# Retention with both heads' zero-padded queries in one full-array product

## The chip, the cores and the metric

The kernel runs on one core of a Trainium2 chip. Its engines are TensorE (PE; its weight loads are shown apart as PEld), VectorE (DVE), ScalarE (ACT), GpSimd (POOL) and SyncE (SP), which here issues nearly all DMA transfers. The metric is the device time of one execution in microseconds: before, the median of three runs is 3554.91 us (3552.26 to 3559.05).

## The reference

A decoder trunk of two layers on a stream of 16 + 512 = 528 positions with 1024 channels. Each layer normalises, projects once, runs four token mixers (RWKV-7, Mamba-2 SSD, retention, RG-LRU), merges them by gates, and ends with a SwiGLU network. Only retention is touched, so only it is shown: 8 heads, keys and queries of 64, values of 128, chunks of positions.

```python
q = rope(q.reshape(bsz, t_len, H, DK), pos)
k = rope(k.reshape(bsz, t_len, H, DK), pos) * (DK ** -0.5)
...
scores = jnp.einsum('bclhd,bcshd->bchls', qc, kc) * intra
y_in = jnp.einsum('bchls,bcshe->bclhe', scores, vc)
kv = jnp.einsum('bclhd,hl,bclhe->bchde', kc, k_dec, vc)

def step(r_state, kv_c):
    return chunk_dec * r_state + kv_c, r_state

_, r_prev = lax.scan(step, jnp.zeros(...), jnp.moveaxis(kv, 1, 0))
y_x = jnp.einsum('bclhd,hl,cbhde->bclhe', qc, q_dec, r_prev)
y = (y_in + y_x).reshape(bsz, nc * L, H, DV)[:, pad:]
y = y * lax.rsqrt(jnp.mean(y * y, axis=-1, keepdims=True) + NORM_EPS)
return jax.nn.silu(g) * y.reshape(bsz, t_len, RET_V_WIDTH)
```

`rope` rotates pairs of channels by the position, `intra` is a causal mask with a decay per head, and `r_prev` is the state of 64 x 128 that a head hands from chunk to chunk.

## The kernel before, in words

All activations are kept transposed: channels on partitions, the 528 positions along the free dimension. A projection (`dense`, line 240) multiplies a 1024 x 128 block of weights with the stream. Weights and activations are each split into a rounded part and a remainder (tiles `whi` and `wlo`, `hh` and `hl`), so that each of eight blocks takes three products, on two halves of 264 columns. These dense products make up most of TensorE's work. The small products of the mixers are plain float32; each of those is issued as two instructions, so one such product counts as 2 in the timeline and as 1 in the order.

The order of the work is set by `layer`. RWKV-7 is a serial loop over eight pairs of heads. Each step builds products (line 853), inverts small triangular matrices on VectorE (lines 903 and 905, 31 rounds), sends the result through DRAM (lines 906, 912, 913), brings it back to TensorE (line 936), and runs a chain over nine chunks (lines 955, 960, 971) to the outputs (lines 988, 990). Between the parts, `fill` pulls pieces from a generator `others`, which runs the other mixers and the gates. Each piece ends with a `yield` of its estimated microseconds, and `fill` pulls until its share is used up. A scheduler then orders the instructions by priority; reads of PSUM are marked `soon()` and go ahead. Each engine works through its own list in order.

Retention is the generator `ret`, one call for two heads (j = 0 to 3 in each of two layers, eight units in all). It uses six chunks of 88 positions.

- `rope` (lines 388 to 404) makes the rotated keys `kr` and queries `qr`, with the decay multiplied in (line 401). Two heads of 64 channels share the 128 partitions: head e has rows 64e to 64e + 63.
- `transposes` (line 414) makes `kT` and, per head, `vT`, positions on partitions.
- Scores, line 458: per head and chunk a product of 64 rows, 88 by 88. Line 461 applies the causal mask.
- States, line 471: per chunk and head a product into 64 of the 128 partitions; lines 476 to 479 form the running state `R` on VectorE.
- Outputs, lines 490 and 492: per head and chunk, values times scores (88 rows) plus state times query (64 rows), accumulated in one PSUM region. `group` holds the instructions of one bank in order.
- Line 496 squares the output, line 497 multiplies it by the gate, `sums` (lines 279 to 285) adds the squares over partitions with a rounded part and a remainder, lines 500 and 502 turn the sum into a reciprocal root, line 503 applies it, and `spill` writes the result to DRAM.

The second half runs for one head completely before the other. Its small products go through `psm`, a pool of two PSUM banks, which other parts use too.

Of the kernel before, what the change touches and what calls it, by code (L numbers as in the profile page):

```python
# [21 lines left out]
T = 528  # L22
H2 = 264
# [6 lines left out]
CL = 88  # L30
NC = 6

RWKV0, SSM0, RET0, LRU0, GATE0 = 0, 3328, 6416, 9488, 11536
# [56 lines left out]
class _Em:  # L90
# [294 lines left out]
        o, w = COFF[name] - NCST0, dict(CCOLS)[name]  # L385
        return self.rc[rows, o:o + w]

    def rope(self, ps, p, tag, dec, j):
        nc = self.nc
        x = self.t(p, T, "rx", bufs=1)  # L390
        xs = self.t(p, T, "rxs", bufs=1)
        with self.soon():
            nc.scalar.activation(v2(x), ps, AF.Copy)
        for b in range(4):
            o = (b ^ 1) * 32
            nc.sync.dma_start(out=xs[b * 32:b * 32 + 32], in_=x[o:o + 32])
        r = self.t(p, T, tag)
        nc.vector.tensor_tensor(out=x, in0=x, in1=self.rcc("cos"), op=MUL)
        nc.vector.tensor_tensor(out=xs, in0=xs, in1=self.rcc("sin"), op=MUL)
        nc.vector.tensor_tensor(out=x, in0=x, in1=xs, op=ADD)  # L400
        nc.vector.tensor_tensor(
            out=r.rearrange("p (c x) -> p c x", c=NC), in0=x.rearrange("p (c x) -> p c x", c=NC),
            in1=self.rcc(dec)[:, j * CL:(j + 1) * CL].unsqueeze(1).broadcast_to([128, NC, CL]), op=MUL)
        return r

    def transposes(self, src, use):

        nc = self.nc
        k = src.shape[0]
        for a in range(2):  # L410
            ps = self.bank(self.psm)[:CL, :3 * k]
            for c in range(3):
                o = (3 * a + c) * CL
                nc.tensor.transpose(ps[:, c * k:c * k + k], src[:, o:o + CL], self.c("ident")[:k, :k])  # L414
            with self.soon():
                use(ps, a)

    def ret(self, l, j, X, p, out):
        nc = self.nc
        src = ("w_in", l)  # L420
        kr = self.rope(self.dense(src, RET0 + 512 + j * 128, X), p, "kr", "kdec", j)
        yield DENSE
        qr = self.rope(self.dense(src, RET0 + j * 128, X), p, "qr", "qdec", j)
# [17 lines left out]
        kT = self.t(p, [NC, 128], "kT", parts=CL)  # L441

        def halfview(t, a):
            return t[:, 3 * a:3 * a + 3].rearrange("p c x -> p (c x)")

        self.transposes(kr, lambda ps, a: nc.scalar.activation(halfview(kT, a), ps, AF.Copy))
        vTs, scs = [], []
        for e in range(2):
            vT = self.t(p, [NC, 128], f"vT{e}", parts=CL)
            self.transposes(vs[e], lambda ps, a: nc.scalar.activation(halfview(vT, a), ps, AF.Copy))  # L450
            vTs.append(vT)
            sc = self.t(p, T, f"sc{e}", parts=CL)
            hr = slice(e * 64, e * 64 + 64)
            for a in range(2):
                ps = self.bank(self.psm)[:CL, :H2]
                for c in range(3):
                    o = a * H2 + c * CL
                    nc.tensor.matmul(ps[:, c * CL:(c + 1) * CL], kr[hr, o:o + CL], qr[hr, o:o + CL],
                                     start=True, stop=True)
                with self.soon():  # L460
                    nc.vector.tensor_tensor(
                        out=sc[:, a * H2:(a + 1) * H2].rearrange("p (c x) -> p c x", c=3),
                        in0=ps.rearrange("p (c x) -> p c x", c=3),
                        in1=self.c("cau", slice(0, CL)).unsqueeze(1).broadcast_to([CL, 3, CL]), op=MUL)
            scs.append(sc)
            yield 2.2
        R = self.t(p, [NC, 128], "R")
        for c in range(NC - 1):
            ps = self.bank(self.psm)[:, :128]
            for e in range(2):  # L470
                nc.tensor.matmul(ps[e * 64:e * 64 + 64], kT[:, c, e * 64:e * 64 + 64], vTs[e][:, c],
                                 start=True, stop=True)
            cd = self.rcc("cdec")[:, j:j + 1]
            with self.soon():
                if c == 0:
                    nc.vector.tensor_scalar(out=R[:, 1], in0=ps, scalar1=cd, scalar2=None, op0=MUL)
                else:
                    nc.vector.tensor_tensor(out=R[:, c + 1], in0=R[:, c], in1=ps, op=ADD)
                    nc.vector.tensor_scalar(out=R[:, c + 1], in0=R[:, c + 1], scalar1=cd, scalar2=None, op0=MUL)
        for e in range(2):  # L480
            hr = slice(e * 64, e * 64 + 64)
            y = self.t(p, T, "rx", bufs=1)
            sq = self.t(p, T, "rxs", bufs=1)
            for a in range(2):
                ps = self.bank(self.psm)[:, :H2]
                for i in range(3):
                    c = 3 * a + i
                    o = ps[:, i * CL:(i + 1) * CL]
                    cs = slice(c * CL, (c + 1) * CL)
                    fs = [lambda: nc.tensor.matmul(o, vTs[e][:, c], scs[e][:, cs], start=(c == 0), stop=True)]  # L490
                    if c:
                        fs.insert(0, lambda: nc.tensor.matmul(o, R[hr, c], qr[hr, cs], start=True, stop=False))  # L492
                    self.group(fs, i > 0)
                ts = slice(a * H2, (a + 1) * H2)
                with self.soon():
                    nc.scalar.activation(sq[:, ts], ps, AF.Square)
                    nc.vector.tensor_tensor(out=y[:, ts], in0=ps, in1=gs[e][:, ts], op=MUL)
            room = [self.t(p, T, tag, dt=F32R) for tag in ("kr", "qr")] if e else [
                self.t(p, [NC, 128], "kT", dt=F32R).rearrange("p c x -> p (c x)")[:, :T], self.t(p, T, "rv", bufs=2, dt=F32R)]
# [5 lines left out]
            yield 3.0  # L505

    def group(self, fs, after=False):

# [750 lines left out]
def v2(ap):  # L1259

    return ap.rearrange("p (h t) -> p h t", h=2 if ap.shape[-1] == T else 1)
# [73 lines left out]
```

## Time and profile before

| what | value |
|---|---|
| median of three runs | 3554.91 us |
| profiled execution | 3565.17 us, span 3563.4 us |
| mean granted clock of TensorE | 0.978 of full |
| TensorE busy | 3456.8 us (97%) |
| VectorE busy | 2396.1 us (67%) |
| ScalarE busy | 1542.5 us (43%) |
| GpSimd busy | 185.6 us (5%) |

TensorE is busy nearly all the time; the others are beside it. In a timeline row the first number is the start in us from the start of the span, the second the time until the last of the merged products has drained. Products overlap in the array, so the cost of a product in a stream is the distance between starts, not the second number.

### The profile page before, as it was taken

How to read it: one execution, taken by the hardware profiler on the slowest of the kernel's cores; microseconds unless marked ns; L12 is line 12 of the kernel's file. 1: busy time of each engine (PE TensorE's matmuls, PEld its weight loads, DVE VectorE, ACT ScalarE, POOL GpSimd, SP SyncE). 2: the span in 40 equal slices, each digit the busy share in tenths (PEclk: the TensorE clock that was granted, in tenths of full speed). 3: DMA queues.
4: the chain of work that ended last, by engine and by line, in shares of the span. 5: the costliest groups of instructions: out<-in, count | busy, mean ns of one | idle time of the engine just before them, and what ended most of it. 6: DMA issues, size and time to landing. Idle time of an engine off the chain costs nothing. (4 is left out here: it accounts for less than half of the span.)

```text
span 3563.4 us, 61528 instructions
## 1 busy us (share of the span) xinstructions
PE 3456.8 (97%) x24768; PEld 3141.3 (88%) x24768; DVE 2396.1 (67%) x4628; ACT 1542.5 (43%) x2272; POOL 185.6 (5%) x477
## 2 busy tenths in 40 slices
PE   8999999999999999999999998999999999999998
PEld 7999989899998999999988887889888887788887
DVE  8877776686897555544348788678768886555533
ACT  6655444445445334222246565445444353332222
POOL 1000100100000000000000001010000000000001
PEclk9999999999999999999999998999999999999999
DMA  4333222222224553233333233222323235533232
GB/s 132 99 100 96 94 83 83 77 87 83 85 85 136 160 174 106 89 91 100 118 105 108 91 97 99 73 81 93 91 71 91 80 114 167 177 116 95 95 97 87
DMA packets 171742, 365.52 MB, mean 103 GB/s; under 512 B 54880, under 2 KB 63712, under 8 KB 171456
## 3 DMA queue, kind: packets, MB, share of 16 engines
q1 hardware_dynamic: 169936, 360.09, 32.6%
q8 instruction: 196, 3.21, 0.4%
q10 hardware_dynamic: 1152, 1.05, 0.1%
q14 instruction: 90, 0.74, 0.1%
q0 software_dynamic: 368, 0.44, 0.0%
HBM read 309.47 MB, written 47.71 MB: 100 GB/s over the span
## 5 line engine op out<-in xcount | busy, mean ns | idle before, releaser
L240 PE MATMUL d<-hh,whi 128*128 128x264 f32 (+1 forms) x4928 | 1189.0, 309 | 23.8 <-ACT whi L217 9.6
L240 PE MATMUL d<-hl,whi 128*128 128x264 f32 (+1 forms) x4928 | 1188.6, 308 | 1.1 <-DVE hl L259 1.0
L240 PE MATMUL d<-hh,wlo 128*128 128x264 f32 (+1 forms) x4928 | 1180.5, 307 | 0.7 <-DVE wlo L218 0.6
L217 ACT ACTIVATE whi<-raw 128x1024 fp32r<-128x1024 f32 (+1 forms) x462 | 485.6, 1051 | 1155.2 <-PE d L240 909.2
L240 PEld LDWEIGHTS d<-hh,whi 128*128 128x128 f32 x4928 | 808.5, 192 | 64.0 <-ACT whi L217 9.6
L240 PEld LDWEIGHTS d<-hl,whi 128*128 128x128 f32 x4928 | 807.3, 191 | 35.7 <-DVE hl L259 2.3
L240 PEld LDWEIGHTS d<-hh,wlo 128*128 128x128 f32 x4928 | 805.5, 191 | 33.2 <-issue 2.2
L218 DVE TENSOR_TENSOR wlo<-raw,whi 128x1024 fp32r<-128x1024 f32 (+1 forms) x462 | 561.3, 1215 | 282.8 <-ACT whi L217 259.7
L240 PE MATMUL d<-yh,whi 128*128 128x264 f32 (+1 forms) x768 | 206.0, 324 | 5.1 <-ACT yh L258 5.1
L240 PE MATMUL d<-yl,whi 128*128 128x264 f32 (+1 forms) x768 | 208.0, 324 | 0.5 <-DVE yl L259 0.5
L240 PE MATMUL d<-yh,wlo 128*128 128x264 f32 (+1 forms) x768 | 206.7, 323 | 0.0
L903 DVE TENSOR_TENSOR sm<-E,NS 36x31 f32<-36x31 f32 (+15 forms) x496 | 164.1, 331 | 14.5 <-DMA E<-xd 5.0
L905 DVE TENSOR_TENSOR NS<-NS,sm 36x31 f32<-36x31 f32 (+15 forms) x496 | 164.3, 331 | 10.0
L240 PEld LDWEIGHTS d<-yh,whi 128*128 128x128 f32 x768 | 126.6, 188 | 19.7 <-ACT yh L258 9.1
L240 PEld LDWEIGHTS d<-yl,whi 128*128 128x128 f32 x768 | 127.9, 188 | 13.4 <-DVE yl L259 2.0
L240 PEld LDWEIGHTS d<-yh,wlo 128*128 128x128 f32 x768 | 127.6, 188 | 11.0
L240 PE MATMUL d<-fh,whi 128*128 128x264 f32 (+1 forms) x506 | 132.3, 318 | 0.0
L240 PE MATMUL d<-fl,whi 128*128 128x264 f32 (+1 forms) x506 | 132.0, 317 | 0.0
L240 PE MATMUL d<-fh,wlo 128*128 128x264 f32 (+1 forms) x506 | 131.5, 316 | 0.0
L1167 DVE TENSOR_TENSOR fg<-d,nr 128x528 f32<-128x528 f32 (+1 forms) x44 | 30.8, 700 | 125.8 <-PE d L240 122.4
L1050 DVE SCALAR_TENSOR_TENSOR gth<-gth,d 128x528 f32<-128x528 f32 (+1 forms) x48 | 33.4, 696 | 99.4 <-PE d L240 99.3
L1172 DVE TENSOR_TENSOR fth<-d,fth 128x528 f32<-128x528 f32 (+1 forms) x44 | 30.8, 700 | 92.6 <-PE d L240 92.5
(604 smaller groups left out, 4786.2 us busy)
## 6 DMA issues: line engine op xcount, KB each, us to landing
raw<-w SPq DMA_DIRECT2D x462, 512.0 KB
g<-gth SPq DMA_DIRECT2D x32, 264.0 KB
Bs<-acd SPq DMA_DIRECT2D x32, 264.0 KB
gth<-g SPq DMA_DIRECT2D x32, 264.0 KB
g<-gth SPq DMA_DIRECT2D x32, 256.0 KB
gth<-g SPq DMA_DIRECT2D x32, 256.0 KB
yd<-lt SPq DMA_DIRECT2D x16, 264.0 KB
ya<-wy SPq DMA_DIRECT2D x16, 264.0 KB
```

The lines of the kernel that those rows point to most:

```text
L217: nc.scalar.activation(hi[:, :n], raw[:, :n], AF.Copy)
L218: nc.vector.tensor_tensor(out=lo[:, :n], in0=raw[:, :n], in1=hi[:, :n].bitcast(F32), op=SUB)
L240: nc.tensor.matmul(ps[:, h], w[:, k - k0], xv[:, h], start=(k == 0 and w is hi and xi == 0), stop=(k == nk - 1 and w is lo))
L903: nc.vector.tensor_tensor(out=pr, in0=X3[:, :a, a:a + 1].broadcast_to([nl, a, w]), in1=N3[:, a:a + 1, a:].broadcast_to([nl, a, w]), op=MUL)
L905: nc.vector.tensor_tensor(out=N3[:, :a, a:], in0=N3[:, :a, a:], in1=pr, op=ADD)
L1050: nc.vector.scalar_tensor_tensor(out=v2(th), in0=v2(th), scalar=1.0, in1=pz, op0=ADD, op1=MUL)
L1167: nc.vector.tensor_tensor(out=v2(g), in0=pg, in1=v2(r), op=MUL)
L1172: nc.vector.tensor_tensor(out=v2(th), in0=pu, in1=v2(th), op=MUL)
```

## The change

Retention is computed with other products.

- The query tile gets a second half: for each chunk there are two copies of 88 columns, one with the rows of head 0 and zeros in the other 64 rows, one with those of head 1. Two half-height instructions on VectorE (line 412 after) and two memsets on GpSimd (line 411) make it where one instruction did before.
- One product per chunk then gives the scores of both heads: all 128 rows of `kr` against 176 columns (line 469), in place of two products with 64 rows and 88 columns. The mask is applied to two chunks and two heads at once.
- The sixth chunk of the keys is no longer transposed, since no state follows it. The state products (line 479) are the same 10 products of two instructions; four chunks share one PSUM bank, the fifth has its own.
- The outputs (lines 493, 496) of both heads are made together: per chunk one product of the whole state `R` (128 rows) with the 176 query columns, then one product of values and scores per head. A bank holds two chunks of both heads; squares and gated outputs of both heads are read from it in four instructions.
- The sums over partitions and the final scaling follow for both heads behind one another; the gated output is written over the gate tile. Other dead tiles serve as room for the rounded parts.
- The estimates at the yields are cut differently, with the same sum of 10.4.

The diff at its core:

```diff
-    def rope(self, ps, p, tag, dec, j):
+    def rope(self, ps, p, tag, dec, j, pair=False):
...
-        nc.vector.tensor_tensor(
-            out=r.rearrange("p (c x) -> p c x", c=NC), in0=x.rearrange("p (c x) -> p c x", c=NC),
-            in1=self.rcc(dec)[:, j * CL:(j + 1) * CL].unsqueeze(1).broadcast_to([128, NC, CL]), op=MUL)
+        r = self.t(p, [NC, 2, CL], tag)
+        for e in range(2):
+            hr, opp = slice(e * 64, e * 64 + 64), slice(64 - e * 64, 128 - e * 64)
+            nc.gpsimd.memset(r[opp, :, e], 0.0)
+            nc.vector.tensor_tensor(out=r[hr, :, e], in0=x3[hr], in1=d3[hr].broadcast_to([64, NC, CL]), op=MUL)
         return r
...
-        vTs, scs = [], []
...
-                for c in range(3):
-                    o = a * H2 + c * CL
-                    nc.tensor.matmul(ps[:, c * CL:(c + 1) * CL], kr[hr, o:o + CL], qr[hr, o:o + CL],
+        sc = self.t(p, [NC, 2, CL], "sc", parts=CL)
+        cau = self.c("cau", slice(0, CL)).unsqueeze(1).unsqueeze(1).broadcast_to([CL, 2, 2, CL])
+        for c0 in range(0, NC, 2):
+            ps = self.bank(self.psm)[:CL, :4 * CL].rearrange("p (c e x) -> p c e x", c=2, e=2)
+            for c in range(c0, c0 + 2):
+                nc.tensor.matmul(ps[:, c - c0], kr[:, c * CL:(c + 1) * CL], qz[:, c], start=True, stop=True)
+            with self.soon():
+                nc.vector.tensor_tensor(out=sc[:, c0:c0 + 2], in0=ps, in1=cau, op=MUL)
...
+        for c0, n in ((0, 4), (4, 1)):
+            ps = self.bank(self.psm)[:, :n * 128].rearrange("p (c x) -> p c x", c=n)
+            for c in range(c0, c0 + n):
+                for e in range(2):
+                    nc.tensor.matmul(ps[e * 64:e * 64 + 64, c - c0], kT[:, c, e * 64:e * 64 + 64], vTs[e][:, c],
                                      start=True, stop=True)
...
-                    fs = [lambda: nc.tensor.matmul(o, vTs[e][:, c], scs[e][:, cs], start=(c == 0), stop=True)]
-                    if c:
-                        fs.insert(0, lambda: nc.tensor.matmul(o, R[hr, c], qr[hr, cs], start=True, stop=False))
-                    self.group(fs, i > 0)
+                fs = [] if c == 0 else [lambda: nc.tensor.matmul(ps[:, c - c0], R[:, c - 1], qz[:, c],
+                                                                start=True, stop=False)]
+                for e in range(2):
+                    fs.append(lambda e=e: nc.tensor.matmul(ps[:, c - c0, e], vTs[e][:, c], sc[:, c, e],
+                                                           start=(c == 0), stop=(c == 0 or e == 1)))
+                self.group(fs, c > c0)
+            ts = slice(c0 * CL, (c0 + 2) * CL)
+            with self.soon():
+                for e in range(2):
...
+                    nc.scalar.activation(c2(sqs[e]), ps[:, :, e], AF.Square)
+                    nc.vector.tensor_tensor(out=c2(gs[e]), in0=ps[:, :, e], in1=c2(gs[e]), op=MUL)
```

The order on TensorE in the first unit of the first layer, scores and states, before (`cst` is the identity of the transposes, `d` the PSUM tile of a dense product, `s` a bank of `psm`; x6 means six products):

```order
L458 MATMUL s<-qr,kr 88x88 x6
L240 MATMUL d<-hh,wlo 128x264
L240 MATMUL d<-hh,whi 128x264 x2
L414 MATMUL s<-cst,rv 88x128 x6
L240 MATMUL d<-hl,whi 128x264 x2
L458 MATMUL s<-qr,kr 88x88 x6
L240 MATMUL d<-hh,wlo 128x264 x2
L240 MATMUL d<-hh,whi 128x264
L471 MATMUL s<-vT_5535,kT 64x128
L471 MATMUL s<-vT_5557,kT 64x128
L240 MATMUL d<-hh,whi 128x264
L240 MATMUL d<-hl,whi 128x264
```

The same place after, where the lines 469 and 479 are the scores and the states:

```order
L469 MATMUL s<-qr,kr 88x176 x4
L240 MATMUL d<-hl,whi 128x264 x2
L240 MATMUL d<-hh,wlo 128x264
L469 MATMUL s<-qr,kr 88x176 x2
L479 MATMUL s<-vT_5537,kT 64x128
L479 MATMUL s<-vT_5548,kT 64x128
L479 MATMUL s<-vT_5537,kT 64x128
```

The two bursts of six score products have become four and two wider ones, and the pairs of state products, which stood between dense products, are now ten in a row.

The outputs of the first head in the same unit on TensorE, before, with 88 rows in line 490 and 64 in line 492:

```order
L490 MATMUL s<-sc_5546,vT_5535 128x88
L492 MATMUL s<-qr,R 128x88
L490 MATMUL s<-sc_5546,vT_5535 128x88
L492 MATMUL s<-qr,R 128x88
L490 MATMUL s<-sc_5546,vT_5535 128x88
L240 MATMUL d<-hh,wlo 128x264
L240 MATMUL d<-hh,whi 128x264
L492 MATMUL s<-qr,R 128x88
```

And after, for both heads, with 128 rows in line 493 and 88 in line 496:

```order
L496 MATMUL s<-sc,vT_5537 128x88
L496 MATMUL s<-sc,vT_5548 128x88
L493 MATMUL s<-qr,R 128x176
L496 MATMUL s<-sc,vT_5537 128x88
L496 MATMUL s<-sc,vT_5548 128x88
L240 MATMUL d<-hl,whi 128x264
L493 MATMUL s<-qr,R 128x176
L496 MATMUL s<-sc,vT_5537 128x88
L496 MATMUL s<-sc,vT_5548 128x88
```

The alternation of two kinds of row counts is gone, and a chunk of both heads takes three products for four.

## Rows read from the trace of the kernel before

**Rows 1.** the page, busy time of each engine (us, share of span, instructions)
```profile
PE 3456.8 (97%) x24768; PEld 3141.3 (88%) x24768; DVE 2396.1 (67%) x4628; ACT 1542.5 (43%) x2272; POOL 185.6 (5%) x477
```

**Rows 2.** timeline of TensorE, second head: start, length until drained, products merged
```profile
486.82 0.35 PE L490 MATMUL s<-sc,vT 88*128 88x88 f32 x2
487.10 0.45 PE L492 MATMUL s<-qr,R 64*128 64x88 f32 x2
487.49 0.46 PE L490 MATMUL s<-sc,vT 88*128 88x88 f32 x2
...
490.80 0.49 PE L240 MATMUL d<-hh,wlo 128*128 128x264 f32 x2
```

**Rows 3.** timeline of TensorE, RWKV outputs of the first step
```profile
166.16 0.39 PE L988 MATMUL s<-MR,XK 128*128 128x128 f32 x2
166.38 0.39 PE L990 MATMUL s<-AR,SV 128*128 128x128 f32 x2
```

**Rows 4.** seven stretches: length, busy PE PEld DVE ACT POOL, clock, DMA share, GB/s
```profile
605.30:608.70 3.40, 3.40 (x17) 3.36 (x16) 2.41 (x6) 1.34 (x3) 0.00 (x0) 0.50 0.21 81
...
sum 40.90, PE 40.90 PEld 34.75 DVE 20.91 ACT 18.73 POOL 0.00; mean PE 5.84 PEld 4.96 DVE 2.99 ACT 2.68 POOL 0.00
```

**Rows 5.** timeline of TensorE in and after a stretch of rows 4
```profile
714.12 0.64 PE L240 MATMUL d<-hh,whi 128*128 128x264 f32 x2
714.56 0.64 PE L240 MATMUL d<-hl,whi 128*128 128x264 f32 x2
...
718.27 0.41 PE L240 MATMUL d<-hh,wlo 128*128 128x264 f32 x2
718.51 0.41 PE L240 MATMUL d<-hh,whi 128*128 128x264 f32 x2
```

**Rows 6.** groups by shape, line 490 on TensorE: busy us, mean ns
```profile
L490 PE MATMUL s<-sc,vT 88*128 88x88 f32 x192 | 45.5, 321 | 1.4 <-ACT rxs L500 1.4
```

**Rows 7.** timeline of TensorE, scores of one head
```profile
466.30 0.28 PE L240 MATMUL d<-hh,wlo 128*128 128x264 f32 x1
466.54 1.17 PE L458 MATMUL s<-qr,kr 64*88 64x88 f32 x12
467.64 0.39 PE L240 MATMUL d<-hh,wlo 128*128 128x264 f32 x1
467.86 0.28 PE L240 MATMUL d<-hh,whi 128*128 128x264 f32 x1
```

**Rows 8.** timeline of TensorE, RWKV score products of 256 columns
```profile
444.00 1.89 PE L853 MATMUL s<-AR,bk 128*128 128x256 f32 x8
445.54 0.47 PE L240 MATMUL d<-hh,whi 128*128 128x264 f32 x1
```

**Rows 9.** timeline of TensorE, one burst of state products
```profile
470.62 0.28 PE L240 MATMUL d<-hh,whi 128*128 128x264 f32 x1
470.83 0.44 PE L471 MATMUL s<-vT,kT 88*64 88x128 f32 x4
...
471.43 0.28 PE L240 MATMUL d<-hl,whi 128*128 128x264 f32 x1
```

**Rows 10.** timeline of TensorE, two such bursts in a row
```profile
2398.69 0.66 PE L471 MATMUL s<-vT,kT 88*64 88x128 f32 x8
2399.28 0.50 PE L240 MATMUL d<-hl,whi 128*128 128x512 f32 x1
```

**Rows 11.** line 401, the decayed query on VectorE: ns min/median/max
```profile
L401 DVE TENSOR_TENSOR qr<-rx,rc x8: 698/708/710, 450.3 to 2573.0; 128x528 f32<-128x528 f32 x8
```

**Rows 12.** same table, eight retention units, transposes to outputs
```profile
463.40:490.70 27.30, 27.21 (x199) 22.76 (x198) 22.18 (x61) 11.46 (x19) 0.00 (x0) 1.00 0.19 59
...
sum 236.70, PE 234.72 PEld 184.82 DVE 145.63 ACT 107.52 POOL 11.09; mean PE 29.34 PEld 23.10 DVE 18.20 ACT 13.44 POOL 1.39
```

**Rows 13.** timeline of TensorE, a wait for the RWKV inverse
```profile
2215.14 1.17 PE L936 MATMUL s<-sm,XK 32*32 32x32 f32 x18 [11.42 <-DVE ends L542]
```

**Rows 14.** line 490, weight loads on TensorE: ns min/median/max
```profile
L490 PEld LDWEIGHTS s<-sc,vT x192: 186/189/333, 476.1 to 2640.8; 88*128 88x128 f32 x192
```

More of the change, by code (lines that the diff above doesn't have):

```diff
@@ L396, in rope @@
             nc.sync.dma_start(out=xs[b * 32:b * 32 + 32], in_=x[o:o + 32])
-        r = self.t(p, T, tag)
         nc.vector.tensor_tensor(out=x, in0=x, in1=self.rcc("cos"), op=MUL)
@@ L400, in rope, with transposes @@
         nc.vector.tensor_tensor(out=x, in0=x, in1=xs, op=ADD)
-        nc.vector.tensor_tensor(
-            out=r.rearrange("p (c x) -> p c x", c=NC), in0=x.rearrange("p (c x) -> p c x", c=NC),
-            in1=self.rcc(dec)[:, j * CL:(j + 1) * CL].unsqueeze(1).broadcast_to([128, NC, CL]), op=MUL)
+        x3 = x.rearrange("p (c x) -> p c x", c=NC)
+        d3 = self.rcc(dec)[:, j * CL:(j + 1) * CL].unsqueeze(1)
+        if not pair:
+            r = self.t(p, T, tag)
+            nc.vector.tensor_tensor(out=r.rearrange("p (c x) -> p c x", c=NC), in0=x3,
+                                    in1=d3.broadcast_to([128, NC, CL]), op=MUL)
+            return r
+        r = self.t(p, [NC, 2, CL], tag)
[3 more added lines that the diff above has]
+            nc.vector.tensor_tensor(out=r[hr, :, e], in0=x3[hr], in1=d3[hr].broadcast_to([64, NC, CL]), op=MUL)
         return r
-    def transposes(self, src, use):
+    def transposes(self, src, use, chunks=NC):
         nc = self.nc
@@ L410, in transposes @@
         for a in range(2):
-            ps = self.bank(self.psm)[:CL, :3 * k]
-            for c in range(3):
+            n = min(3, chunks - 3 * a)
+            ps = self.bank(self.psm)[:CL, :n * k]
+            for c in range(n):
                 o = (3 * a + c) * CL
@@ L422, in ret @@
         yield DENSE
-        qr = self.rope(self.dense(src, RET0 + j * 128, X), p, "qr", "qdec", j)
+        qz = self.rope(self.dense(src, RET0 + j * 128, X), p, "qr", "qdec", j, pair=True)
         yield DENSE
@@ L440, in ret, with view @@
             yield DENSE
[L441 to L446, printed above, removed]
-        vTs, scs = [], []
+        kT = self.t(p, [NC - 1, 128], "kT", parts=CL)
+        def view(t, a):
+            return t[:, 3 * a:min(3 * a + 3, t.shape[1])].rearrange("p c x -> p (c x)")
+        self.transposes(kr, lambda ps, a: nc.scalar.activation(view(kT, a), ps, AF.Copy), NC - 1)
@@ L448, in ret @@
+        vTs = []
         for e in range(2):
             vT = self.t(p, [NC, 128], f"vT{e}", parts=CL)
-            self.transposes(vs[e], lambda ps, a: nc.scalar.activation(halfview(vT, a), ps, AF.Copy))
+            self.transposes(vs[e], lambda ps, a: nc.scalar.activation(view(vT, a), ps, AF.Copy))
             vTs.append(vT)
[L452 to L456, printed above, removed]
-                    o = a * H2 + c * CL
-                    nc.tensor.matmul(ps[:, c * CL:(c + 1) * CL], kr[hr, o:o + CL], qr[hr, o:o + CL],
-                                     start=True, stop=True)
[L460 to L473, printed above, removed]
-            with self.soon():
[L475 to L479, printed above, removed]
@@ L480, in ret @@
-        for e in range(2):
[L481 to L489, printed above, removed]
-                    fs = [lambda: nc.tensor.matmul(o, vTs[e][:, c], scs[e][:, cs], start=(c == 0), stop=True)]
-                    if c:
-                        fs.insert(0, lambda: nc.tensor.matmul(o, R[hr, c], qr[hr, cs], start=True, stop=False))
-                    self.group(fs, i > 0)
[L494 to L499, printed above, removed]
+        yield 2.2
@@ new lines, in ret @@
+        R = self.t(p, [NC - 1, 128], "R")
+        cd = self.rcc("cdec")[:, j:j + 1]
+        for c0, n in ((0, 4), (4, 1)):
[3 more added lines that the diff above has]
+                    nc.tensor.matmul(ps[e * 64:e * 64 + 64, c - c0], kT[:, c, e * 64:e * 64 + 64], vTs[e][:, c],
+                                     start=True, stop=True)
+            with self.soon():
+                for c in range(c0, c0 + n):
+                    if c == 0:
+                        nc.vector.tensor_scalar(out=R[:, 0], in0=ps[:, 0], scalar1=cd, scalar2=None, op0=MUL)
+                    else:
+                        nc.vector.tensor_tensor(out=R[:, c], in0=R[:, c - 1], in1=ps[:, c - c0], op=ADD)
+                        nc.vector.tensor_scalar(out=R[:, c], in0=R[:, c], scalar1=cd, scalar2=None, op0=MUL)
@@ new lines, in ret, with c2 @@
+        yield 2.2
+        sqs = [self.t(p, T, tag, bufs=1) for tag in ("rx", "rxs")]
+        for c0 in range(0, NC, 2):
+            ps = self.bank(self.psm)[:, :4 * CL].rearrange("p (c e x) -> p c e x", c=2, e=2)
+            for c in range(c0, c0 + 2):
+                fs = [] if c == 0 else [lambda: nc.tensor.matmul(ps[:, c - c0], R[:, c - 1], qz[:, c],
[7 more added lines that the diff above has]
+                for e in range(2):
+                    def c2(t):
+                        return t[:, ts].rearrange("p (c x) -> p c x", c=2)
+                    nc.scalar.activation(c2(sqs[e]), ps[:, :, e], AF.Square)
+                    nc.vector.tensor_tensor(out=c2(gs[e]), in0=ps[:, :, e], in1=c2(gs[e]), op=MUL)
@@ L500, in ret @@
+        yield 4.0
+        for e in range(2):
+            sq, y = sqs[e], gs[e]
+            if e:
+                room = self.t(p, T, "kr", dt=F32R), self.t(p, T, "rv", bufs=2, dt=F32R)
+            else:
+                x = self.t(p, [2, T], "qr", dt=F32R)
+                room = x[:, 0], x[:, 1]
             self.sums(self.psm, 0, [(sq, *room)], lambda ps, ts: nc.scalar.activation(
@@ L504, in ret @@
             out.append(self.spill("yc", 2 * j + e, y))
-            yield 3.0
+        yield 2.0
     def group(self, fs, after=False):
```

## The prediction

> **What bounds the kernel now.** I read the page first, then the groups of instructions by shape, then the timeline of TensorE around one retention unit, and last the table of stretches. The page's line of engines shows the matmul side of TensorE (PE) busy for 3456.8 of 3563.4 us [rows 1]. A busy PE is not a fast one, though: a product counts as busy while it drains, so what a product costs has to be read from the distance between starts on the timeline.
>
> A retention unit is one turn of the generator `ret` (two heads); there are four in each of two layers, eight in all. In its last stage the products of line 490 (weights: 88 rows of the transposed values) and of line 492 (weights: 64 rows of the state) take turns. Each timeline row there is one float32 product, issued as two instructions. From the first row at 486.82 to the dense product at 490.80 one head takes 3.98 us for 22 instructions; a row in the middle takes 0.38 to 0.39 us, 0.19 per instruction [rows 2]. Lines 988 and 990 of the RWKV part do the same kind of pair, with longer products (128 columns), and take 0.22 us for two instructions [rows 3]. The difference between the two places is that 988 and 990 both use 128 rows, whereas 490 and 492 use a different number of rows each time. I read this as a change of the array's row setting at every row of the timeline, with nothing overlapped across it.
>
> The same stage drags the clock. Seven stretches that begin inside or just after this stage have a granted clock of 0.50, the 1.2 GHz level, 40.9 us together [rows 4]. A pair of dense products there takes 0.44 us, against 0.24 at full clock [rows 5]. By group, the 192 instructions of line 490 alone are busy 45.5 us [rows 6].
>
> **The change, part by part.** Durations are from the profiled execution, 3565.17 us with its span of 3563.4; the three timed runs have a median of 3554.91, 10.3 us less, so I carry the difference over to the median.
>
> *Second stage of the products (lines 490, 492; new 493, 496).* Per unit now: 2 heads x 3.98 = 7.96 us. After: both heads share one state product of 128 rows by 176 columns per chunk (5 chunks, 10 instructions), and there are 24 instructions for the two heads' score-by-value products of 88 columns, as before. All of them use 128 weight columns and the full row setting. A 128-column instruction costs 0.11 us [rows 3]; for 88 columns I take 0.11 too, since the nearest cheaper row, 0.09 for 88 columns with 88 weight columns, is the lower bound [rows 7]. A 176-column instruction lies between 0.09 (88 columns [rows 7]) and 0.19 (256 columns: eight in 1.54 us [rows 8]); I take the middle, 0.15. Sum: 10 x 0.15 + 24 x 0.11 = 4.14, a gain of 3.82 per unit.
>
> *Scores (line 458; new 469).* Now 12 instructions of one head in a burst: from the dense product at 466.30 to the next but one at 467.86 it is 1.56 us, less two dense products of 0.12 [rows 5, 7], so 1.32, and twice per unit 2.63. After: 12 instructions of 176 columns, 1.80. Gain 0.83.
>
> *States (line 471; new 479).* Now five bursts of four instructions, each between dense products: 470.62 to 471.43 is 0.81 [rows 9], less two dense 0.24, so 0.57, and five make 2.83. Eight in a row took 0.59 (2398.69 to 2399.28), 0.074 each [rows 10]. So going into and out of the burst of four costs 0.57 - 0.30 = 0.27, and after, with all 20 in a row (the order shows that), 20 x 0.074 + 0.27 = 1.75. Gain 1.08, at least nothing.
>
> *One transposition less* per unit, and no copy of the sixth chunk: left at nothing.
>
> *Clock.* If the stage no longer leaves the array half idle, the 40.9 us at 1.2 GHz shrink by 1 - 0.24/0.44 = 0.45 of it: 18.6 us, a little less since not all in them is dense; 18. Bounds: 0 and 18.6. I take 18, since in each of the eight units nothing but this stage leaves the array so empty. Low stretches outside retention are left as they are.
>
> Sum: (3.82 + 0.83 + 1.08) x 8 = 45.8, plus 18, is 63.8 us of PE time.
>
> *What is added.* VectorE: the decayed query is written as two half-height instructions, each at most as long as the present one of 0.71 us [rows 11], so 0.71 more per unit, 5.7 in all; the gated output reads PSUM 12 times in smaller pieces for 8 now (ScalarE's square and VectorE's product each). GpSimd: two memsets per unit on an engine that is 5% busy [rows 1], and the query tile that they write is long free. SyncE: the two spills of a unit stand side by side; the weight loads queued behind them have three buffers of lead. All this lies beside PE: over the eight stretches of retention PE is busy 234.7 of 236.7 us and VectorE 145.6 [rows 12]. Taking 63.8 off the one and adding 5.7 to the other leaves 170.9 against 151.3, so PE still ends last on the sum. It does not in each stretch: in the first, VectorE has 22.18 us and PE 27.21 [rows 12], and PE less 5.7 is below it. There the stall goes over to VectorE.
>
> *What is late next.* Each RWKV chunk set has an inverse on VectorE, whose result goes through DRAM and is then wanted by line 936; dense and retention work fills PE meanwhile. If that filler is too short PE stands, as at 2215.14, where it waited 11.42 us [rows 13]. Shorter retention work is shorter filler. The new order already moves some dense rows ahead of line 936. I count four fifths of the 63.8 as reaching the end: 51. So 3565 - 51 = 3514 for a profiled execution, and 3554.9 - 51 = 3504 for the median.
>
> **The rivals.**
>
> *The inverse takes over.* The filler of the affected RWKV steps gets some 6 to 8 us shorter and PE reaches line 936 before VectorE is through. For it: the 11.42 us wait [rows 13], and a VectorE that is nearly the longer engine in the first stretch. Against it: in the retention stretches PE has hardly any idle time [rows 12], so it is PE that the others wait for. It leaves two fifths: 26 us, 3529.
>
> *Everything arrives, and stalls go along.* The joined stage turns its PSUM banks over less often (three times for scores where there were four, two for states where there were five). The whole 63.8 and up to 20 more by fewer stalls: about 3483.
>
> *The clock stays low.* If something else in these stretches holds the clock down, the sum is 45.8, four fifths of it 37: 3518. Against it: each of the seven low stretches begins in or right behind the stage with alternating rows [rows 4, 5].
>
> *Weights are not hidden (slower).* The new stage has 46 large instructions per unit, each with its own weights; should a load wait for the product before it, its own 0.19 us [rows 14] stands on the path. The second stage is then 10 x (0.15 + 0.19) + 24 x (0.09 + 0.19) = 10.1 us per unit for 7.96, and the scores 12 x 0.34 = 4.1 for 2.63; with states 1.08 better that is 2.5 x 8 = 20 slower: 3575. It decides from about 0.17 us exposed per instruction (63.8 / 368). Against it: the products of lines 988 and 990 have weights of the same 128 columns in the same row setting and start 0.11 apart, less than one load [rows 3]. The Trainium skill (TensorE: Matmul & The Clock Gate, Part 3: Packing small matmuls — row/col tiling) states this rule: weight loads overlap running products only where the row group differs, which here it would not. The trace disagrees with it [rows 3].
>
> *Padding wastes the array (slower for the scores).* The heads' score products have 64 rows each, and padding gives up running them side by side. The Trainium skill (TensorEngine Tiling (Array Packing), When to Use Tiling) would pair them, twice as fast. By that rule the present scores would cost 12 x 0.09 = 1.1 per unit, and the change would lose 0.7 x 8 = 6 us there where I count 7 gained; the sum would be 51, its four fifths 41. In the trace they are not paired: 12 of one head stand in one burst and take 1.10 us [rows 7].
>
> **How the numbers follow.** My forecast, 3504 with 3492 to 3517 of its own, has 0.70. The inverse as bound has 0.12, all and more 0.10, the clock staying low 0.05, weights exposed 0.03. The bounds of the 176-column instruction (0.09 to 0.19; 176 of them) are worth 10 us less and 7 us more. To leave out no more than 2 in 10 the range goes from 3478 to 3532. This kernel's measurement tells about 0.2%, 7 us, from no change. Faster by more than that: all but the exposed weights and the end of the inverse case, 0.95; within: 0.02; slower: 0.03.
>
> **What would show it.** On the timeline after, line 493 followed by two rows of 496 should take about 0.75 us per chunk for both heads (two rows of each head now take 1.5), and dense products after the stage 0.24 a pair, with the granted clock at 1.00 in the eight units. The 20 instructions of line 479 should take 1.5 us in a row. It would be wrong if line 493 and 496 start 0.18 us or more apart, if the granted clock falls after the stage again, or if PE waits for several us before line 950 (936 now) in the steps that hold retention work.

## The result and the profile after

The changed kernel takes 3507.77 us (median of 4 runs, 3503.01 to 3509.68) against 3556.24 for the kernel before (4 runs, 3552.26 to 3559.05). The ratio is 0.9863, 95% interval 0.9849 to 0.9876: 48 us less. The forecast was 3504, 51 us less. The profiled execution took 3509.68 us with a span of 3507.9 and a mean granted clock of 0.982 (before: 3565.17, 3563.4 and 0.978); between these two executions the difference is 55 us. Left out of all medians and ratios below is one execution of `e9_before_grouped`, which took 3686.85 us at a mean granted clock of 0.842, where its other five had 0.982 to 0.985.

The page's line of engines, which answers to [rows 1]:

```profile
PE 3393.5 (97%) x24584; PEld 3108.5 (89%) x24584; DVE 2397.0 (68%) x4644; ACT 1535.4 (44%) x2284; POOL 191.6 (5%) x493
```

TensorE is as full as before, 97%. Its busy time, with what the low clock adds to it, became shorter by 63.3 us, and its idle time longer by 7.8 (106.6 to 114.4), which together gives the 55 us. VectorE's busy time stayed the same. Next the output stage of the first unit on TensorE's timeline (start, length until drained, products merged). It answers to [rows 2]; line 493 is the new joined state product, line 496 the old line 490:

```profile
474.04 0.58 PE L496 MATMUL s<-sc,vT 88*128 88x88 f32 x4
474.46 0.50 PE L493 MATMUL s<-qr,R 128*128 128x176 f32 x2
...
475.16 0.36 PE L240 MATMUL d<-hl,whi 128*128 128x264 f32 x1
475.36 0.46 PE L493 MATMUL s<-qr,R 128*128 128x176 f32 x2
...
476.07 0.50 PE L493 MATMUL s<-qr,R 128*128 128x176 f32 x2
476.40 0.58 PE L496 MATMUL s<-sc,vT 88*128 88x88 f32 x4
476.77 0.49 PE L240 MATMUL d<-hh,wlo 128*128 128x264 f32 x2
477.09 0.40 PE L240 MATMUL d<-hh,whi 128*128 128x264 f32 x2
...
477.45 0.53 PE L493 MATMUL s<-qr,R 128*128 128x176 f32 x2
...
478.93 0.37 PE L240 MATMUL d<-hl,whi 128*128 128x264 f32 x1
479.14 0.40 PE L240 MATMUL d<-hh,wlo 128*128 128x264 f32 x2
479.38 0.40 PE L240 MATMUL d<-hh,whi 128*128 128x264 f32 x2
```

Read the starts, not the lengths. A chunk of both heads goes from 476.07 to 476.77, 0.70 us; before, two heads took 1.5 for it. The four instructions of line 496 take 0.37 us, 0.09 each, where those of line 490 took 0.19. The dense pairs behind the stage stand 0.24 apart, which is the full clock of [rows 5].

The scores (line 469) and states (line 479) of the same unit, which answer to [rows 7] and [rows 9]:

```profile
466.46 0.49 PE L240 MATMUL d<-hh,whi 128*128 128x264 f32 x2
467.00 1.40 PE L469 MATMUL s<-qr,kr 128*88 128x176 f32 x8
468.11 0.53 PE L240 MATMUL d<-hl,whi 128*128 128x264 f32 x2
468.47 0.28 PE L240 MATMUL d<-hh,wlo 128*128 128x264 f32 x1
468.59 0.76 PE L469 MATMUL s<-qr,kr 128*88 128x176 f32 x4
469.28 1.31 PE L479 MATMUL s<-vT,kT 88*64 88x128 f32 x20
470.52 0.39 PE L240 MATMUL d<-hh,wlo 128*128 128x264 f32 x1
```

All 20 state instructions go in 1.24 us, without the way back to dense work; before, five bursts took 0.57 each, with it.

The clock: the table of stretches, here for the eight retention units from their first transposition to the last output product (us, busy PE PEld DVE ACT POOL, granted clock, DMA share, GB/s). It answers to [rows 4] and [rows 12], with the first row and the sum:

```profile
462.70:478.90 16.20, 16.08 (x136) 14.96 (x134) 14.95 (x41) 6.50 (x14) 0.00 (x0) 1.00 0.12 37
...
sum 151.50, PE 150.94 PEld 132.55 DVE 103.96 ACT 66.55 POOL 11.02; mean PE 18.87 PEld 16.57 DVE 13.00 ACT 8.32 POOL 1.38
```

The granted clock is 1.00 in all eight, and none of the seven stretches at 1.2 GHz is left. In the first unit VectorE is at 14.95 of 16.20 us: closer to TensorE, but still not the longer one. The eight stretches are 85 us shorter in sum than those of [rows 12], more than the whole gain: dense work that stood in them now stands elsewhere, so their lengths say nothing of the gain.

What took part of it back is in TensorE's list of waits (us in total, times, longest). First three lines of the kernel before that were not shown yet, then the changed kernel, then its timeline around the longest of the grown waits for the inverse:

```profile
PE s L285 <- ACT v L279: 5.9, 6, 1.7
...
PE s L936 <- DVE sm L927: 4.3, 5, 1.9
...
PE d L240 <- DVE Bs L333: 0.6, 1, 0.6
```

```profile
PE s L950 <- DVE ends L556: 11.4, 1, 11.4
PE s L950 <- DVE sm L941: 10.0, 7, 4.0
PE s L285 <- ACT v L279: 8.8, 9, 1.9
...
PE d L240 <- DVE Bs L333: 4.3, 1, 4.3
```

```profile
502.84 0.97 PE L950 MATMUL s<-sm,XK 32*32 32x32 f32 x18 [4.02 <-DVE sm L941]
...
504.12 0.64 PE L240 MATMUL d<-hh,wlo 128*128 128x264 f32 x2
504.56 0.42 PE L240 MATMUL d<-hh,whi 128*128 128x264 f32 x1
```

Line 950 is the old line 936, the wait for the inverse. The 11.4 us are those of [rows 13]. The others were 4.3 us in five places before and are 10.0 in seven; the longest is 4.02 us where it was 1.9. Behind it a pair of dense products takes 0.44 us again: the clock falls there. Three short stretches of low clock are new, of which this is the first. The second, at 2291.7, follows a wait of 1.86 us in line 285; ahead of the third, at 2527.3, no wait in 15 us is longer than 0.7:

```profile
503.20:506.60 3.40, 3.40 (x22) 2.92 (x19) 2.73 (x5) 0.48 (x1) 0.00 (x0) 0.51 0.45 147
...
sum 10.20, PE 10.08 PEld 9.23 DVE 6.67 ACT 1.80 POOL 0.89; mean PE 3.36 PEld 3.08 DVE 2.22 ACT 0.60 POOL 0.30
```

A fourth one has another wait ahead of it, the longest that is new: at 838.9 us line 240 waits 4.31 us for line 333 on VectorE, which reads a dense product of another mixer out of PSUM. There the granted clock is 0.50 for 6.8 us from 841.1. The kernel before waits 0.6 us for that line. So the new stretches add up to 17.0 us.

### The profile page after: what moved, and what is told of

It is laid out like the page before. It is cut to its first block, busy times and chain, and to the rows that moved or that the text cites. A ratio compares the mean times of both kernels' runs of the same rounds, so it can differ in the third digit from the quotient of the medians.

```text
span 3507.9 us, 61182 instructions
## 1 busy us (share of the span) xinstructions
PE 3393.5 (97%) x24584; PEld 3108.5 (89%) x24584; DVE 2397.0 (68%) x4644; ACT 1535.4 (44%) x2284; POOL 191.6 (5%) x493
```

## The experiments

Two theories were to be told apart. The first is the prediction's: a product that needs another row setting than the one before it pays for the change, and a stage full of such changes pulls the clock down. The rival says that joining both heads and packing the banks is what pays: fewer and larger products, fewer turns of a bank. Every experiment is timed in five rounds against the kernel before on its own chip, so ratios are compared, not times from different chips. "Rows" are rows of the array. Row counts still take turns after the change, 128 and 88; what the first theory needs is that these two share a setting, and that 64 has another.

### The output stage with 64 rows, and with 128

The changed kernel, with its output stage as separate products per head again. `e1_rows64` takes the head's 64 rows; `e2_rows128` differs in one line, and the two traces hold the same 24664 instructions of TensorE in the same order:

```
 for c0 in (0, 3):
     for e in range(2):
-        hr = slice(e * 64, e * 64 + 64)     # e1
+        hr = slice(0, 128)                  # e2
         ps = self.bank(self.psm)[:, :H2]
         for c in range(c0, c0 + 3):
             ...
                 fs.insert(0, lambda: nc.tensor.matmul(o, R[hr, c - 1], qz[hr, c, e], ...))
```

> The changed kernel, but the output stage uses one state product per head with that head's 64 rows (88 columns), alternating with the value products of 88 rows, one bank per head and half. Scores and states stay as changed. If the cost was the change of row setting at every product: the stage goes back from about 4.1 to 8 us per unit and the low clock behind it comes back, so 30 us and up to 18 us, in all 3507.8 + 30 to 48 = 3538 to 3556. If the gain came from having 34 instructions for 44: 44 x 0.11 - 4.1 = 0.7 us per unit, 3513. If it came from making both heads' outputs together, nothing is lost: 3508.

> The same as e1_rows64, instruction for instruction, but the state product of a head takes all 128 rows against the zero-padded query of that head (88 columns). If row settings are the cost: 44 instructions at 0.11 us, 4.8 us per unit against 4.1, so 3507.8 + 6 = 3513, granted clock 1.00 behind the stage. If the number of instructions is the cost: the same time as e1_rows64. If padding wastes the array: no faster than e1_rows64.

Measured: 64 rows 3565.54 us, ratio 1.0031 (1.0019 to 1.0043); 128 rows 3504.83, ratio 0.9853 (0.9837 to 0.9869). TensorE's timeline in the same place of the two, first 64 rows, then 128 (line 498 is the state product, 496 the value product):

```profile
474.18 0.45 PE L498 MATMUL s<-qr,R 64*128 64x88 f32 x2
474.56 0.46 PE L496 MATMUL s<-sc,vT 88*128 88x88 f32 x2
...
482.79 0.73 PE L498 MATMUL s<-qr,R 64*128 64x88 f32 x2
483.45 0.73 PE L496 MATMUL s<-sc,vT 88*128 88x88 f32 x2
```

```profile
468.98 0.39 PE L498 MATMUL s<-qr,R 128*128 128x88 f32 x2
469.20 0.39 PE L496 MATMUL s<-sc,vT 88*128 88x88 f32 x2
```

A product (two instructions) starts 0.38 us after the one before it with 64 rows and 0.22 with 128, with the same columns and weights of the same width: 0.16 us per change. With 64 rows the clock then falls inside the stage, and a product takes 0.66. The eight stretches at 1.2 GHz in or behind the stage, first row and sum:

```profile
479.10:489.30 10.20, 10.20 (x38) 8.86 (x39) 4.70 (x13) 3.24 (x5) 0.00 (x0) 0.50 0.23 78
...
sum 75.00, PE 75.00 PEld 62.08 DVE 35.38 ACT 29.39 POOL 0.84; mean PE 9.38 PEld 7.76 DVE 4.42 ACT 3.67 POOL 0.10
```

So 61 us lie between two kernels that differ in the row count of 80 products, 20 changes of setting in each of eight units. Note the value products: their 88 rows did not change the setting when they alternated with 128 (0.22 us). The direction was as the first theory said; the size was missed. I expected 64 rows to stay below the kernel before, and they came out slightly above it. The low stretches add up to 75.0 us for 40.9 [rows 4], which by the prediction's 0.45 us lost for each is 15 us. Why they are longer is argued, not shown: here both heads' alternating products stand close together, whereas before they came head by head.

The Trainium skill (TensorEngine Tiling (Array Packing), Key Properties) says that a change of tiling mode drains TensorE. The two timelines fit that, with 0.16 us for it here. The Trainium skill (TensorE: Matmul & The Clock Gate, Part 3: Packing small matmuls — row/col tiling) lists that a weight load overlaps a running product only where the row group differs, though the same section, a few lines above, also lets a load into the background weight buffer go ahead of running products. The 128-row kernel disagrees with the list, with products of the full row setting 0.11 us per instruction apart and loads of 0.19 each.

### One part of the change alone, in the kernel before

`e8_before_padded` stores the padded query, leaves the sixth chunk's keys untransposed as the change does, and uses the padded query in the state product; the heads still go one after the other, scores, states and banks stay as before, and some dead tiles serve as room for others:

```
-    fs.insert(0, lambda: nc.tensor.matmul(o, R[hr, c], qr[hr, cs], ...))
+    fs.insert(0, lambda: nc.tensor.matmul(o, R[:, c - 1], qz[:, c, e], ...))
```

> Kernel before with one part of the change alone: the query is stored with the other head's rows at zero, and the product of the running state takes all 128 rows; each head's output stage keeps its place, its banks and its order, and scores and states stay as they were. By the theory that the change of row setting in the output stage is what costs time and clock, this alone must give most of the gain: outputs 30.6 us and clock 18 of the 51 that were forecast, so about 3508 to 3515 us. By the rival that joining both heads and packing the banks is what pays, it stays at 3545 to 3556.

Measured: 3511.44 us (3503.56 to 3516.60), ratio 0.9876 (0.9856 to 0.9896), as the first theory has it. Its timeline, and the eight retention units in the table of stretches:

```profile
470.36 0.39 PE L502 MATMUL s<-qr,R 128*128 128x88 f32 x2
470.59 0.39 PE L500 MATMUL s<-sc,vT 88*128 88x88 f32 x2
```

```profile
460.40:481.30 20.90, 20.89 (x176) 18.81 (x175) 17.71 (x50) 8.25 (x14) 0.00 (x0) 1.00 0.22 65
...
sum 163.40, PE 163.15 PEld 135.55 DVE 108.24 ACT 81.11 POOL 10.18; mean PE 20.39 PEld 16.94 DVE 13.53 ACT 10.14 POOL 1.27
```

The padding alone gives 44 of the 49 us that the ratios of both kernels make of 3556, and their intervals overlap. The clock is 1.00 in all eight units. What joining the heads, packing the banks and the other products add on top is 0.0013 of the ratio, with an uncertainty of about twice that: in time, not shown to be anything.

The clock was not the same, though. Its mean is 0.9868 over the five executions of e8, 0.9807 over the eleven of the kernel before beside it, and 0.9826 over eight of the changed kernel. Between 2.4 and 1.2 GHz that is 93, 137 and 122 us at the lower level (twice the missing share of the span). At 0.45 us lost for each, which is 0.44 against 0.24 us for a pair of dense products [rows 5], the clock gave e8 some 20 of its 44 us, and the changed kernel some 7 of its 48. That leaves 24 and 41 us for shorter work: the other parts of the change probably did shorten the work, by some 17 us, and lost most of that again to low clock. This is an estimate from clocks that are given to 0.001; no run shows it by itself.

### The same instructions in another order

`e9_before_grouped` leaves every product of the kernel before as it is, 64 rows included, and only puts a bank's state products ahead of its value products. The row setting then changes 8 times a unit where it changed 20 times:

```
-    for i in range(3):
-        ... state product of chunk i, then value product of chunk i
+    for st in (0, 1):
+        for i in range(3):
+            if st == 0 and c:
+                ... state product of chunk i, start=(i == 1 - a), stop=False
+            if st:
+                ... value product of chunk i, start=False, stop=(i == 2)
```

> Kernel before, 64-row state products kept, but in each bank the two or three state products come first and the value products after them, so that the row setting changes 8 times a unit where it changed 22 times; the instructions are the same in number and shape. By the theory that the change of row setting is what costs: a product without a change takes 0.22 us (two instructions at 0.11, from the kernel with 128-row state products) and 0.39 with one (68.6 us over 176 products before), so 14 changes at 0.17 us in eight units are 19 us, and up to 18 more where the clock stays up: 3516 to 3537, likeliest 3525. By the rival that a 64-row product that accumulates is slow in itself, however it is ordered: 3550 to 3556.

Measured: 3533.97 us (3527.65 to 3540.56), ratio 0.9929 (0.9908 to 0.9950), which is 25 us of 3556. The 22 changes of the expectation are a miscount: eleven products in turns have ten changes, 20 for two heads, so 12 went and not 14, about 16 us instead of 19 without the clock. TensorE's timeline:

```profile
483.97 0.68 PE L492 MATMUL s<-qr,R 64*128 64x88 f32 x4
484.57 0.90 PE L494 MATMUL s<-sc,vT 88*128 88x88 f32 x6
485.40 0.90 PE L492 MATMUL s<-qr,R 64*128 64x88 f32 x6
486.23 0.90 PE L494 MATMUL s<-sc,vT 88*128 88x88 f32 x6
```

Six instructions take 0.83 us, change included; in the kernel before, six took 1.17, three rows of the timeline at 0.39 [rows 2]. Six at 0.11 would be 0.66, so a change is 0.17 us. Without the 0.11 of the other kernel it comes out the same: 0.83 for six with one change and 0.39 for two with one leave 0.11 per instruction and 0.17 per change. The 64-row product is not slow in itself: the change is. Only two of the low stretches are left in or behind the stage (here the first, then the sum of both):

```profile
2390.80:2394.20 3.40, 3.40 (x10) 2.64 (x9) 3.30 (x9) 0.99 (x3) 0.00 (x0) 0.50 0.21 80
...
sum 6.80, PE 6.80 PEld 5.46 DVE 4.50 ACT 3.40 POOL 0.00; mean PE 3.40 PEld 2.73 DVE 2.25 ACT 1.70 POOL 0.00
```

This is the cleanest test of the cause: the same work, other neighbours, and both time and clock follow. With 12 of the 20 changes gone it brings 25 us, where the padding, which takes away all of them, brings 44.

### Scores back to 64 rows, and side by side

`e3_scores64` undoes the padding in the scores of the changed kernel; `e4_scores_side` also lets the heads take turns, each with its own bank:

```
 e3:  for e in range(2):
          for c0 in (0, 3):
              ps = self.bank(self.psm)[:CL, :H2]...
              for c in range(c0, c0 + 3):
                  nc.tensor.matmul(ps[:, c - c0], kr[hr, c * CL:(c + 1) * CL], qz[hr, c, e], ...)
 e4:  for c0 in (0, 3):
          pss = [self.bank(self.psm)[:CL, :H2]... for _ in range(2)]
          for c in range(c0, c0 + 3):
              for e in range(2):
                  nc.tensor.matmul(pss[e][:, c - c0], kr[hr, ...], qz[hr, c, e], ...)
```

> The changed kernel, but the scores are products of one head with 64 rows and 88 columns again, one head behind the other, four banks; outputs and states stay as changed. By the terms of the prediction (0.83 us per unit): 3507.8 + 7 = 3514. If half as long products make up for their number (24 x 0.08 against 12 x 0.15, without the cost of going in and out of the 64-row setting): 3508.

> Like e3_scores64, but the heads' 64-row products alternate and write two different banks, so that the two halves of the array could work side by side. If they do: 12 pairs at 0.08 us, 1.0 us per unit and some 0.3 for going in and out, against 1.8 now: 3507.8 - 4 = 3504. If they do not: like e3_scores64, 3514.

Measured: 3521.41 us, ratio 0.9906 (0.9887 to 0.9925), and 3527.74, ratio 0.9912 (0.9895 to 0.9929). The scores by shape (busy us, mean ns), first e3, then e4, then the changed kernel's joined ones:

```profile
L471 PE MATMUL s<-qr,kr 64*88 64x88 f32 x192 | 20.6, 249 | 0.0
```

```profile
L471 PE MATMUL s<-qr,kr 64*88 64x88 f32 x192 | 18.7, 254 | 0.0
```

```profile
L469 PE MATMUL s<-qr,kr 128*88 128x176 f32 x96 | 18.4, 317 | 0.1
```

Taking turns is not twice as fast: 18.7 us busy for 20.6, and not less in time. No run here shows two such products side by side. By the Trainium skill (TensorEngine Tiling (Array Packing), When to Use Tiling) products of 64 rows are for row tiling, two at a time. Here the padded product, which spends half its rows on zeros, is as short in TensorE's time and the whole kernel is not slower for it. Undoing the padding here costs about 0.0043 of the ratio, 15 us, more than the 2.2 us of busy time can explain. The wait of line 285 for `v` went from 8.8 to 10.7 us; the rest of the 15 stays open.

### States in single bursts again

`e5_states_single` gathers the state products one chunk per bank, as before the change:

```
-        for c0, n in ((0, 4), (4, 1)):
+        for c0, n in [(c, 1) for c in range(NC - 1)]:
```

> Changed kernel, but with the five state products of each head gathered one chunk per PSUM bank, as in the kernel before, in place of four chunks in one bank and one in the next. If the term for the states (1.08 us a unit, 8.6 us in all) is time on the path, about 3516 us; if the vector engine's chain of state updates, or the wait that follows it, covers the difference, 3508 (3505 to 3511). In the trace the 160 state products took 10.8 us of starts in the changed kernel against 14.6 before, so 4 us is all that TensorE itself can lose; more than that would have to come through the clock.

Measured: 3515.24 us (3503.69 to 3519.65), ratio 0.9879 (0.9859 to 0.9900). That is 0.0016 above the changed kernel, 6 us, on the side of the term's 8.6; but the intervals overlap, so it is not settled.

### Can the waits for the inverse be filled?

`e6_filler` moves 3 us of filler from one share of the planner to another in the changed kernel, and `e7_rows128_filler` does the same in the 128-row kernel:

```
-F1, F2, F3 = 48.0, 33.0, 170.0
+F1, F2, F3 = 51.0, 30.0, 170.0
```

> Changed kernel with one number changed: while the inverse runs, the planner hands out 51 us of other work in the first part and 30 in the second, where it was 48 and 33. If the waits for line 950 (11.4 us in one place, 10.0 us in seven others) and the three short low-clock stretches right behind such waits took back what the prediction left out, about 3500 us; if these waits only stand in for others, 3508 (3505 to 3512).

> The kernel with separate 128-row state products per head and the planner's shares 51 and 30. If the two edits work apart, 3497 (3505 less what the filler gives, forecast at 8); if the waits only move, 3505 (3502 to 3508).

Measured: 3512.95 us, ratio 0.9888 (0.9868 to 0.9908), and 3536.56, ratio 0.9948 (0.9928 to 0.9967). Neither gained: the first is 0.0025 of the ratio above the changed kernel, with the intervals overlapping, and the second 0.0095 above `e2_rows128`, 34 us. The waits for the inverse (line 950 in the first, 948 in the second):

```profile
PE s L950 <- DVE sm L941: 19.7, 6, 11.8
```

```profile
PE s L948 <- DVE sm L939: 24.9, 9, 11.8
```

With the old shares these two kernels waited 21.4 us (11.4 and 10.0) and, by the same view, 16.9. More filler in the first part only moves the wait; in the 128-row kernel it adds 8 us to it. Most of the other 26 us go with the clock: its mean is 0.9785 over the six executions of e7 and 0.9858 over the four of `e2_rows128`, 52 us more at 1.2 GHz, which by the same 0.45 is some 23 us, an estimate. In the trace, for one, 13.7 us at 1.2 GHz begin at 489.2 in a wait of 3.24 us for the inverse. That the waits could be had back cheaply is not shown.

### The two candidates on one chip

Changed kernel and 128-row kernel, both unaltered:

> The changed kernel unaltered, on the same chip as the two others: 3508 (3503 to 3512).

> The kernel with separate 128-row state products per head, unaltered, beside the changed kernel: 3505 if its 3 us are real, 3508 if joining both heads into 176 columns makes no difference to the time.

Measured: 3511.30 us (3504.86 to 3517.60), ratio 0.9863 (0.9842 to 0.9883), and 3505.32 (3501.92 to 3515.11), ratio 0.9850 (0.9829 to 0.9872). The kernel that doesn't join the heads is ahead by 0.0010 and 0.0013 of the ratio, on two chips, with intervals that overlap: not shown to be better, nor worse. That the columns are joined brings no time that these runs show.

## Why the prediction was right

It was 3.8 us from the measured 3507.77, inside its own range, and its main case came true. By its steps:

*What the output stage costs* was right. Forecast 4.14 us per unit; in the unit shown the three pieces take 1.12, 1.41 and 1.48 us, and the three returns to dense work 0.08, 0.08 and 0.09 more than a dense product, together 4.26. The way back to dense work, 0.25 of it, was not in the forecast's sum. The inputs were a little off, against each other: a value product of 88 columns takes 0.09 per instruction (I took 0.11), a joined one of 176 columns 0.16 (476.07 to 476.40 holds two; I took 0.15).

*The reason* was right, and is shown three ways: by row count alone (61 us), by the padding alone (44 of 49), and by order alone (25).

*Scores and states*: the states' 20 instructions take 1.24 us for 1.5 expected. The scores' bursts take 1.11 and 0.69 us, the 1.80 forecast to the digit, but without the way in from the dense product at 466.46 and back; with it they come to 2.22 in this unit, so the 0.83 was too much here. What they are worth in time depends on what stands around them: undone one by one in the changed kernel they cost 15 us (intervals apart) and 6 (overlapping); left out together, in the padded kernel before, they and the joining come to 5, with the intervals overlapping. So in time these two terms do not add up as a sum per unit has it; by the estimate under e8 the work did become shorter, and the clock took most of it back.

*The clock* was right in its place and too large in sum. All seven stretches went, worth 18.6 us at most by the sum of the prediction. The four new ones of 17.0 us give back 17.0 x 0.45 = 7.7 at most (in the fourth TensorE stands still for 2.1 us). Over the executions whose clock is on record its mean is 0.9805 for the kernel before (39) and 0.9826 for the changed one (8): 139 and 122 us at 1.2 GHz, 17 less, worth some 7 us and not 18. I had not foreseen that a wait of a few us can be followed by low clock: that adds to the price of a wait.

*Four fifths arriving* came out by the number, 48 of 63.8 by the medians, and this was partly luck. If the clock gave 7 of the 48, the shorter work gave some 41 of the 45.8 it was put at, nine tenths; the fifth that was taken off stands mostly for a clock term that was too large. The two profiled executions show the same from another side: TensorE's busy time fell by 63.3 us, about the sum, and 7.8 of it came back as idle time. The reason given for the loss holds: waits for the inverse grew by 5.7 us, those of line 285 for `v` by 2.9 and the one for line 333 by 3.7, while others became shorter. The rival of the inverse was thus no invention, but came in at a quarter of its price. What the prediction listed as a sign against it, waits of several us before line 950, did appear (4.02 us) beside its success. The stall that was to go over to VectorE in the first stretch did not: TensorE is busy for 16.08 of 16.20 us there.

*The other rivals* fell. The stalls did not go along, since idle time grew. In the eight units the clock stayed up; no weights were exposed (line 496 at 0.09 us per instruction); the scores' padding did not cost (undoing it costs 15 us).

## What to carry to other kernels

Look for places where small products of different row counts take turns on TensorE, and compare start to start with a neighbour of one row count: here a change cost 0.16 to 0.17 us, and a stage full of changes brought the clock down behind it. Bring the products to one row setting with zeros, or, where that can't be done, group those of one setting: the first gave 44 us here and the second 25. Don't count on larger products for their own sake, and don't take a sum of small savings for time: the parts beside the output stage, worth some 15 us by the sum, could not be told from nothing in time. Compare the mean granted clock of two kernels before you compare their times: a few us of new waits, with low clock behind them, can eat what shorter work saved.

## What was not expected of the hardware

The prediction took it for granted that products of 88 rows have the full row setting; that this is so was seen only afterwards. Products of 88 rows between products of 128 rows cost no change (0.11 us per instruction), products of 64 rows between those of 88 did. So it was not any difference in row count that cost; which counts share a setting was seen only for these three.

One and the same kernel can have a stretch at 1.2 GHz in one execution and none in another. The same 13.7 us of the 128-row kernel, well ahead of its first retention unit, in two executions:

```profile
377.00:390.70 13.70, 13.56 (x145) 12.66 (x144) 12.00 (x27) 5.48 (x8) 2.46 (x2) 1.00 0.27 79
```

```profile
377.00:390.70 13.70, 13.70 (x115) 13.03 (x113) 6.60 (x14) 4.32 (x5) 2.46 (x2) 0.50 0.13 38
```

The first execution has a span of 3503.3 us and the second 3513.3. The same holds for the kernel before: of its 17 executions beside e1, one with a mean clock of 0.984 took 3543.33 us and one with 0.977 took 3564.29, which is 21 us for 51 more at 1.2 GHz. Differences of under 10 us between single profiles of the 128-row kernel can therefore come from the clock alone, and a sum over one trace of each kernel should not be read closer than that.
